# Masking in the scan of a stick-breaking mixer, and transposes in halves of 64 rows, in a two-layer decoder kernel

## The chip, the cores and the metric

The kernel runs on one core of a Trainium2 chip. A core has a matrix engine (TensorE, PE in the profile; its weight loads are listed apart as PEld), a vector engine (VectorE, DVE), a scalar engine (ScalarE, ACT), a general engine (GpSimd, POOL) and a queue engine that starts transfers (SyncE, SP). Each takes its instructions in order from a queue of its own and waits on semaphores for results of the others. Operands lie in SBUF; TensorE writes to PSUM, which has 8 banks of 128 partitions by 512 fp32 numbers, and ScalarE and VectorE read them from there. The metric is the device time of one execution in microseconds; lower is better.

## What is computed

A decoder of two layers on 512 tokens with 1024 features, all in float32. Each layer is a feed-forward half step, a mixer and a second feed-forward half step, each on a normed input; a final norm closes it. The first layer's mixer is a gated linear attention, the second one's (the one changed here) a stick-breaking attention of 16 heads with 64 features. The part that the change touches, cut to its core:

```python
z = jnp.einsum('bhtd,bhsd->bhts', q_blk, k).astype(jnp.float32) * scale
mask = s_pos[None, :] < t_pos[:, None]
sp = jnp.where(mask, jax.nn.softplus(z), 0.0)
rem = lax.cumsum(sp, axis=3, reverse=True) - sp
weights = jnp.where(mask, jnp.exp(jax.nn.log_sigmoid(z) - rem), 0.0)
return jnp.einsum('bhts,bhsd->bhtd', weights.astype(v.dtype), v)
```

A token t may look at tokens s < t alone. Since log_sigmoid(z) = z - softplus(z), the exponent is z minus the sum of softplus from s up to t - 1, taken from the right. For the second edit only the end matters: the last feed-forward half step is added to x, and each token's row is divided by its root mean square and scaled by `final_norm`.

## The kernel before

**Layout.** Activations lie feature by feature: `xs[0..7]`, each 128 features by 512 tokens. A float32 product is made of three products in a rounded format: an operand is cut into a high part (ScalarE's cast, L152 for weights `wh`) and a remainder (VectorE's subtraction, L153, `wl`), and `mm3` adds high x high, low x high and high x low. So each weight tile costs ScalarE and VectorE an instruction before TensorE can use it. Weights come from HBM through SP's queue.

**Order.** The program is a list of entries in `feed.q`, each a generator that issues some products and yields (a "half"). `feed.halves(k)` runs k such pieces, and starting an entry cuts the weights of the next ones ahead of their use. The engines' queues are filled by the framework, which places instructions by their dependences and priorities; `tc.issue_after` holds an instruction behind another. PSUM banks come from four rotating sets ("a" 2 banks, "z" 3, "t" 2, "o" 1). Where no set is named they rotate through all 8, so that the ninth request takes the bank of the first.

**The mixer (class SB).** `run` goes through 17 steps. Step s < 16 makes the logits of one head (`weights_log`); step s > 0 makes the weights of the head of the step before (`weights`: transposes, Exp), and every second step the products with the values (`values`) of a pair of heads. Between them `feed.halves` puts pieces of the projection products that make the next heads' queries, keys and values. So TensorE alternates between a head's own work and projections.

A head's logits (512 queries by up to 512 keys, causal) lie in three banks: `bk` 1 holds query tile 2 (384 columns), `bk` 2 the tiles 1 and 0 (384), `bk` 0 tile 3 (512). For each bank:

- TensorE: two products per query tile (L1484 in `logits`, key high and key low), and a mask product: `idb` (identity, bf16) times `negm` (-1e30 at and right of the diagonal), which adds the mask to the diagonal 128 x 128 block. In steps 0 to 4 it comes behind the logits; from step 5 on (`AHEAD`) `masks` lays the masks of banks 1 and 2 for the next step ahead, as the first write of the bank.
- ScalarE: `l` = |z| (L1527), Exp(-l) and Ln(1 + l) (both through `act`, L656), and `r` = Relu(z) (L1530). r + l is softplus(z), and 0 where masked.
- VectorE: the scan (L1533) runs from right to left in SBUF, state = (r + state) + l, one for each query tile; then r = z - l (L1541), z once more from PSUM, which is the exponent.

`st["relu"]` marks the last Relu; `parts` places the casts of later queries and keys (`mq`, `kh`, L1478) behind it. `weights` then transposes r (L1555, `ps_T`), takes Exp (`wt`) and `values` multiplies (L1570, `ps_oT`).

**The end.** `to_tokens` runs in the last feed-forward half step, ahead of its last product `back_tok` (`ps_bt`). It turns `xs` from feature by feature to token by token: for each half of the features (`hf`) it takes four banks, one for each token tile i, transposes 4 x 4 blocks of 128 x 128 with the block as the stationary operand and `ident` as the moving one (L1650), and ScalarE copies each bank of 512 columns (L1655) into `xt[i, hf]`, which takes the place of `xs`. The first `ps_bt` is the ninth request and takes the first of these eight banks. `last` (L1665) adds the product to `xt`.

Of the kernel before, what the change touches and what calls it, by code (L numbers as in the profile page):

```python
# [23 lines left out]
NT = T // P  # L24
EPS = 1e-6
LEVELS = (64, 32, 16, 8, 4, 2, 1)
NEG = -1.0e30

def turns(t):

    return t.rearrange("p (two n) -> p n two", two=2)
# [13 lines left out]
def decoder(ctx: ExitStack, tc: tile.TileContext, a: dict, out: bass.AP):  # L47
    nc = tc.nc
# [28 lines left out]
    xs = [xp.tile([P, T], F32, name=f"x{k}") for k in range(KD)]  # L77
# [449 lines left out]
    st = {}  # L527
# [102 lines left out]
    def two_halves(between=None):  # L630

        feed.finish()
        g = [feed.start(), feed.start()]
        for i in range(3):
            for n, x in enumerate(g):
                next(x, None)
                next(x, None)
                if between is not None and (i, n) == (1, 0):
                    between((recent[-4], recent[-1]))

    def new_norm():
        st["h"], st["l"], st["made"] = st["nh"], st["nl"], range(KD)
# [6 lines left out]
    def exp_ln_tables(after):  # L649
        with tc.issue_after(after):  # L650
            st["tab"] = nc.scalar.preload_act_table_set("natural_log_exp_and_others").ins

    def act(o, i, fn, **kw):

        with tc.issue_after(st["tab"]):
            st["last"] = nc.scalar.activation(o, i, fn, **kw).ins  # L656
# [744 lines left out]
    class SB:  # L1401
# [81 lines left out]
        def logits(self, o_, l_, r_, first, last=False):  # L1483
            nc.tensor.matmul(o_, l_, r_, start=first, stop=last, skip_group_check=True)  # L1484

        def mask(self, bk, ps, first):

            w = self.WID[bk]
            m0 = P if bk == 2 else w - P
            nb = (w - m0) // P  # L1490
            self.logits(
                ps[:, m0:w].rearrange("p (n s) -> p n s", n=nb),
                self.idb,
                self.negm.unsqueeze(1).to_broadcast([P, nb, P]),
                first,
                not first,
            )

        def masks(self, s):


            if self.AHEAD <= s < 16:
                for bk in (1, 2):
                    self.zs[bk] = psum("ps_z", "z")
                    self.mask(bk, self.zs[bk], True)

        def weights_log(self, p, e):

            m = self.qk[p, e, "q"]
            kh, kl = self.qk[p, e, "k"]  # L1510
            self.ys[p, e] = ys = [None] * 3
            for bk, tiles in ((1, (2,)), (2, (1, 0)), (0, (3,))):
                ahead = bk in self.zs
                ps = self.zs.pop(bk) if ahead else psum("ps_z", "z")
                w = self.WID[bk]
                for n_, i in enumerate(tiles):

                    c0, n = self.BK[i][1], max(2, i + 1) * P
                    ts_ = slice(i * P, (i + 1) * P)
                    o_, h_, l_ = ps[:, c0 : c0 + n], turns(kh)[:, 0 : n // 2], turns(kl)[:, 0 : n // 2]  # L1520
                    self.logits(o_, m[:, ts_], h_, n_ == 0 and not ahead)
                    self.logits(o_, m[:, ts_], l_, False, ahead and i == tiles[-1])
                if not ahead:
                    self.mask(bk, ps, False)
                r = self.hp.tile([P, w], F32, tag=f"r{bk}", name="r")
                l = self.hp.tile([P, w], F32, tag=f"l{bk}", bufs=1, name="l")
                nc.scalar.activation(l, ps[:, 0:w], AF.Abs)  # L1527
                act(l, l, AF.Exp, scale=-1.0)
                act(l, l, AF.Ln, bias=1.0)
                st["relu"] = nc.scalar.activation(r, ps[:, 0:w], AF.Relu).ins  # L1530
                for i in tiles:
                    c = slice(self.BK[i][1], self.BK[i][1] + (i + 1) * P)
                    nc.vector.tensor_tensor_scan(  # L1533
                        out=l[:, c][:, ::-1],
                        data0=r[:, c][:, ::-1],
                        data1=l[:, c][:, ::-1],
                        initial=0.0,
                        op0=ALU.add,
                        op1=ALU.add,
                    )  # L1540
                nc.vector.tensor_tensor(out=r, in0=ps[:, 0:w], in1=l, op=ALU.subtract)  # L1541
                ys[bk] = r
                yield

# [38 lines left out]
        def run(self):  # L1583
            with ExitStack() as es:
                vp = es.enter_context(tc.tile_pool(name="vp2", bufs=1, reuse_waits="tile"))
                self.op = es.enter_context(tc.tile_pool(name="op", bufs=8, reuse_waits="tile"))
                self.qp = es.enter_context(tc.tile_pool(name="qp2", bufs=4, reuse_waits="tile"))
                self.hp = es.enter_context(tc.tile_pool(name="hp3", bufs=2, reuse_waits="tile"))
                self.v = [vp.tile([P, D], F32, name=f"w{i}") for i in range(NT)]
                self.ys, self.wt, self.zs = {}, {}, {}  # L1590
                self.later, self.hold = [], False
                self.idb = vp.tile([P, P], BF16, name="idb")
                self.negm = vp.tile([P, P], BF16, name="negm")
                nc.vector.tensor_copy(self.idb, ident)
                nc.gpsimd.dma_start(self.negm, a["c_neg"])
                new_norm()
                two_halves()
                stats_a("t")
                feed.step(2)
                stats_b("t")  # L1600
                exp_ln_tables(st["sqrt"])
                flush(self.defer)
# [37 lines left out]
    xt = {}  # L1640

    def to_tokens(tp):
        st["tp"] = tp
        fin = st["fin"] = tp.tile([P, D], F32, tag="s", bufs=4, name="fin")
        nc.gpsimd.dma_start(fin, a["final_norm"].partition_broadcast(P))
        for hf in range(2):
            ps = [psum("ps_T") for _ in range(NT)]
            for m in range(4):
                for i in range(NT):
                    nc.tensor.transpose(  # L1650
                        ps[i][:, m * P : (m + 1) * P], xs[hf * 4 + m][:, i * P : (i + 1) * P], ident
                    )
            for i in range(NT):
                xt[i, hf] = xs[hf * 4 + i]
                nc.scalar.copy(xt[i, hf], ps[i])  # L1655

        with tc.issue_after(st["updated"]):
            nc.vector.tensor_scalar(out=fin, in0=fin, scalar1=2.0 * float(D) ** 0.5, scalar2=None, op0=ALU.mult)
# [308 lines left out]
def _constants():  # L1967
# [29 lines left out]
```

## Time and profile before

| what | value |
|---|---|
| three runs, median (lowest to highest) | 1760.18 us (1759.73 to 1760.69) |
| the profiled execution: time, span | 1759.99 us, 1758.0 us |
| granted TensorE clock, mean | 0.999 |
| busy over the span: PE, DVE, ACT, POOL | 99%, 86%, 61%, 3% |
| the mixer's first and last logits (L1484) | 1220.5 and 1384.7 us |
| transposes of the end (L1650), 32 | 1726.8 to 1730.2 us |

The profile is of one execution. Times in it count from the start of the span. A busy share says how long an engine had an instruction in work; matmuls overlap their neighbours, so their distance from start to start is their cost, not their duration. The "chain of waits" follows the work back from the last instruction to what released it. In a row of groups, "x48 | 25.4, 529" is the count, the busy time in us and the mean in ns, and behind the second bar stands the idle time of the engine in front of these instructions and who ended it.

### The profile page before, as it was taken

What the parts mean: (1) busy time and instruction counts of PE and PEld (TensorE: products, weight loads), DVE (VectorE), ACT (ScalarE), POOL (GpSimd) and SP (SyncE); (2) the same over time, 40 slices, a digit from 0 to 9 for tenths busy, and PEclk for the clock granted to TensorE, in tenths of its full rate; (3) what the DMA queues carried; (4) which work ended last, traced back from release to release, by engine and by line L of the source; (5) the groups of instructions that cost most, each with busy time, mean ns of one, the idle gap of its engine ahead of it and who ended that gap; (6) DMA issues with size and microseconds to landing.
All of it is one profiled execution on the core that took longest, in us unless ns stands there. A gap on an engine that the chain in (4) does not pass through costs nothing.

```text
span 1758.0 us, 31376 instructions
## 1 busy us (share of the span) xinstructions
PE 1746.1 (99%) x12714; PEld 1630.1 (93%) x12714; DVE 1509.0 (86%) x2490; ACT 1064.3 (61%) x1903; POOL 55.6 (3%) x77
## 2 busy tenths in 40 slices
PE   9999999999999999999999999999999999999998
PEld 8999999889888999999989999999888889999997
DVE  8999797786888999889798988977898679998886
ACT  7556555555655556555556555655888755555555
POOL 0000000200000000000000000010000000000000
PEclk9999999999999999999999999999999999999999
DMA  5533435412123433444434334352212234434351
GB/s 168 156 112 118 131 110 144 120 56 82 57 93 99 132 109 121 120 121 127 134 94 133 106 123 135 101 132 84 85 49 73 72 96 133 132 97 125 117 148 51
DMA packets 186388, 193.14 MB, mean 110 GB/s; under 512 B 4930, under 2 KB 171124, under 8 KB 186244
## 3 DMA queue, kind: packets, MB, share of 16 engines
q1 hardware_dynamic: 177760, 175.91, 32.0%
q0 software_dynamic: 8240, 14.95, 4.7%
q8 instruction: 99, 1.62, 0.4%
q14 instruction: 45, 0.37, 0.1%
q10 hardware_dynamic: 244, 0.29, 0.0%
HBM read 175.17 MB, written 2.10 MB: 101 GB/s over the span
## 4 chain that ended last, share of the span: by engine, by line
PE 90%; DVE 6%; ACT 3%; issue 1%; DMA 1%; DVEq 0%; SPq 0%
PE ps_w L779 21%; PE ps_d L80 15%; PE ps_f L80 15%; PE ps_q L779 10%; PE ps_z L779 5%; PE ps_t L80 5%; PE ps_w L412 5%; PE ps_b L80 4%; PE ps_q L412 2%; DVE wl L153 1%; PE ps_z L1484 1%; PE ps_z L412 1%; PE ps_oT L1570 1%; PE ps_bt L80 1%; PE ps_T L1555 1%
## 5 line engine op out<-in xcount | busy, mean ns | idle before, releaser
L153 DVE TENSOR_TENSOR wl<-raw,wh 128x1024 fp32r<-128x1024 f32 x241 | 255.5, 1061 | 37.6 <-ACT wh L152 36.6
L152 ACT CAST wh<-raw 128x1024 fp32r<-128x1024 f32 x241 | 222.2, 922 | 72.3 <-PE ps_f L80 27.4
L153 DVE TENSOR_TENSOR wl<-s,wh 128x1024 fp32r<-128x1024 f32 x160 | 195.4, 1221 | 66.4 <-ACT wh L152 65.5
L779 PE MATMUL ps_w<-th,wh 128*128 128x256 f32 x864 | 239.1, 277 | 0.3 <-ACT ps_z L807 0.3
L779 PE MATMUL ps_w<-tl,wh 128*128 128x256 f32 x864 | 237.8, 275 | 0.0
L779 PE MATMUL ps_w<-th,wl 128*128 128x256 f32 x864 | 237.8, 275 | 0.0
L152 ACT CAST wh<-s 128x1024 fp32r<-128x1024 f32 x160 | 168.9, 1055 | 6.0 <-DVE s L765 6.0
L779 PEld LDWEIGHTS ps_w<-th,wh 128*128 128x128 f32 x864 | 165.9, 192 | 1.1 <-ACT ps_z L807 0.5
L80 PE MATMUL ps_f<-xh,wh 128*128 128x512 f32 x432 | 166.4, 386 | 0.0
L779 PEld LDWEIGHTS ps_w<-tl,wh 128*128 128x128 f32 x864 | 166.0, 192 | 0.0
L779 PEld LDWEIGHTS ps_w<-th,wl 128*128 128x128 f32 x864 | 165.9, 192 | 0.0
L80 PE MATMUL ps_f<-xh,wl 128*128 128x512 f32 x432 | 164.1, 380 | 0.5 <-DVE wl L153 0.5
L80 PE MATMUL ps_f<-xl,wh 128*128 128x512 f32 x432 | 163.9, 379 | 0.0
L80 PE MATMUL ps_d<-hh,wh 128*128 128x512 f32 x416 | 157.9, 379 | 0.0
L80 PE MATMUL ps_d<-hl,wh 128*128 128x512 f32 x416 | 157.8, 379 | 0.0
L80 PE MATMUL ps_d<-hh,wl 128*128 128x512 f32 x416 | 157.8, 379 | 0.0
L153 DVE TENSOR_TENSOR wl<-rawd,wh 128x1024 fp32r<-128x1024 f32 (+1 forms) x100 | 96.3, 963 | 9.3 <-ACT wh L152 9.3
L807 ACT COPY ps_z<-ps_w 128x256 f32<-128x256 f32 x72 | 26.0, 362 | 118.1 <-PE ps_w L779 117.8
L363 POOL DMA_DIRECT2D x<-d x53 | 45.9, 911 | 1550.3 <-ACT d L362 1092.2
L80 PEld LDWEIGHTS ps_f<-xh,wl 128*128 128x128 f32 x432 | 81.9, 189 | 11.3 <-DVE wl L153 0.9
L80 PEld LDWEIGHTS ps_f<-xl,wh 128*128 128x128 f32 x432 | 81.8, 189 | 11.3
L80 PEld LDWEIGHTS ps_f<-xh,wh 128*128 128x128 f32 x432 | 81.9, 190 | 10.6
(357 smaller groups left out, 5427.8 us busy)
## 6 DMA issues: line engine op xcount, KB each, us to landing
raw<-in_ffn_w_gate_dram SPq DMA_DIRECT2D x43, 1024.0 KB, 5.4
raw<-in_ffn_w_up_dram SPq DMA_DIRECT2D x43, 1024.0 KB, 5.4
rawd<-in_ffn_w_down_dram SPq DMA_DIRECT2D x84, 512.0 KB, 3.8
x<-d POOLq DMA_DIRECT2D x53, 256.0 KB, 4.5
raw<-in_gla_w_in_dram SPq DMA_DIRECT2D x12, 1024.0 KB, 5.3
raw<-in_sb_w_in_dram SPq DMA_DIRECT2D x16, 512.0 KB, 3.7
raw<-in_gla_w_out_dram SPq DMA_DIRECT2D x4, 1024.0 KB, 4.9
raw<-in_sb_w_in_dram SPq DMA_DIRECT2D x4, 1024.0 KB, 5.2
```

The costliest lines, as they stand in the source:

```text
L80: st["pe"] = nc.tensor.matmul(ps, l, r, start=first, stop=last).ins
L152: nc.scalar.copy(h[:, k], part)
L153: nc.vector.tensor_tensor(out=l[:, k], in0=part, in1=h[:, k].bitcast(F32), op=ALU.subtract)
L363: nc.gpsimd.dma_start(xs[k], d, accum_op=ALU.add)
L412: st["pe"] = nc.tensor.matmul(ps, l_, r_, start=first and c + n == 0, stop=c == 1 and n == 2, skip_group_check=True).ins
L779: st["pe"] = nc.tensor.matmul(o, l_, r_, start=first and j + n == 0, stop=j == 3 and n == 2, skip_group_check=True).ins
L807: v["copied"] = nc.scalar.copy(z, w).ins
L1484: nc.tensor.matmul(o_, l_, r_, start=first, stop=last, skip_group_check=True)
L1555: nc.tensor.transpose(ps[:, c0 : c0 + P], ys[yb][:, yc + j * P : yc + (j + 1) * P], ident)
L1570: nc.tensor.matmul(po[e * 64 : e * 64 + 64, j * P : T], self.v[j][:, c : c + 64], self.wt[p, e][bk][:, c0 : c0 + n], start=j == 0, stop=j ...
```

## The change

**Mixer.** The mask products, `idb`, `negm` and its load, `mask` and `masks` are gone. ScalarE copies the logits out of the bank into `r`; VectorE bounds `r` at 44 in place; ScalarE takes `l` = Exp(r) and Ln(1 + l), which is softplus without the detour by |z|. The mask moves into the scan: a new tile `keep` (128 x 512) holds 1 everywhere but for a 0 in each row where s = t - 1, and the scan is state = keep x state + l from the right, starting at 1e30. Up to the diagonal the state stays 1e30, at s = t - 1 it starts anew with l. The exponent r - l is then -1e30 for masked keys. The subtraction reads `r` from SBUF, so the bank is no longer needed after the copy. `parts` now waits for the last Ln.

**End.** A block is transposed in two halves: 64 of its 128 rows (features) by 128 tokens, with 64 x 64 of `ident` as moving operand, into a 128 x 64 piece. The two halves use the upper and the lower 64 partitions of their operands and go to two different banks; a bank holds one half of two token tiles. The loop goes over token tiles first and the four blocks within, and ScalarE makes two copies of 256 columns for a token tile in place of one of 512.

```diff
-        def mask(self, bk, ps, first):
...
-        def masks(self, s):
...
-                ahead = bk in self.zs
-                ps = self.zs.pop(bk) if ahead else psum("ps_z", "z")
+                ps = psum("ps_z", "z")
...
-                    self.logits(o_, m[:, ts_], h_, n_ == 0 and not ahead)
-                    self.logits(o_, m[:, ts_], l_, False, ahead and i == tiles[-1])
-                if not ahead:
-                    self.mask(bk, ps, False)
+                    self.logits(o_, m[:, ts_], h_, n_ == 0)
+                    self.logits(o_, m[:, ts_], l_, False, i == tiles[-1])
...
-                nc.scalar.activation(l, ps[:, 0:w], AF.Abs)
-                act(l, l, AF.Exp, scale=-1.0)
+                nc.scalar.copy(r, ps[:, 0:w])
+                nc.vector.tensor_scalar(out=r, in0=r, scalar1=TOP, scalar2=None, op0=ALU.min)
+                act(l, r, AF.Exp)
                 act(l, l, AF.Ln, bias=1.0)
-                st["relu"] = nc.scalar.activation(r, ps[:, 0:w], AF.Relu).ins
+                st["logs"] = st["last"]
                 for i in tiles:
                     c = slice(self.BK[i][1], self.BK[i][1] + (i + 1) * P)
                     nc.vector.tensor_tensor_scan(
                         out=l[:, c][:, ::-1],
-                        data0=r[:, c][:, ::-1],
+                        data0=self.keep[:, T - (i + 1) * P :][:, ::-1],
                         data1=l[:, c][:, ::-1],
-                        initial=0.0,
-                        op0=ALU.add,
+                        initial=-NEG,
+                        op0=ALU.mult,
                         op1=ALU.add,
                     )
-                nc.vector.tensor_tensor(out=r, in0=ps[:, 0:w], in1=l, op=ALU.subtract)
+                nc.vector.tensor_tensor(out=r, in0=r, in1=l, op=ALU.subtract)
...
-                self.idb = vp.tile([P, P], BF16, name="idb")
-                self.negm = vp.tile([P, P], BF16, name="negm")
-                nc.vector.tensor_copy(self.idb, ident)
-                nc.gpsimd.dma_start(self.negm, a["c_neg"])
+                self.keep = vp.tile([P, T], F32, name="keep")
+                nc.gpsimd.memset(self.keep, 1.0)
+                c = slice(T - P - 1, T - 1)
+                nc.vector.tensor_scalar(
+                    out=self.keep[:, c], in0=ident, scalar1=-1.0, scalar2=1.0, op0=ALU.mult, op1=ALU.add
+                )
...
-                                self.parts(st["relu"])
+                                self.parts(st["logs"])
...
-                            if i == 1:
-                                self.masks(s + 1)
...
-            ps = [psum("ps_T") for _ in range(NT)]
-            for m in range(4):
-                for i in range(NT):
-                    nc.tensor.transpose(
-                        ps[i][:, m * P : (m + 1) * P], xs[hf * 4 + m][:, i * P : (i + 1) * P], ident
-                    )
+            ps = [psum("ps_T").rearrange("p (i m c) -> p i m c", i=2, c=64) for _ in range(NT)]
+            halves = slice(0, 64), slice(64, P)
+            for i in range(NT):
+                for m in range(4):
+                    x = xs[hf * 4 + m][:, i * P : (i + 1) * P]
+                    for n, r in enumerate(halves):
+                        nc.tensor.transpose(ps[i // 2 * 2 + n][:, i % 2, m], x[r], ident[r, r])
             for i in range(NT):
                 xt[i, hf] = xs[hf * 4 + i]
-                nc.scalar.copy(xt[i, hf], ps[i])
+                to = xt[i, hf].rearrange("p (m n c) -> p n m c", n=2, c=64)
+                for n in range(2):
+                    nc.scalar.copy(to[:, n], ps[i // 2 * 2 + n][:, i % 2])
```

More of the change, by code (lines that the diff above doesn't have):

```diff
@@ L27 @@
 NEG = -1.0e30
+TOP = 44.0
 def turns(t):
@@ L1484, in logits @@
             nc.tensor.matmul(o_, l_, r_, start=first, stop=last, skip_group_check=True)
-        def mask(self, bk, ps, first):
[L1488 to L1496, printed above, removed]
-            )
-        def masks(self, s):
[L1502 to L1505, printed above, removed]
         def weights_log(self, p, e):
@@ L1589, in run @@
                 self.v = [vp.tile([P, D], F32, name=f"w{i}") for i in range(NT)]
-                self.ys, self.wt, self.zs = {}, {}, {}
+                self.ys, self.wt = {}, {}
                 self.later, self.hold = [], False
-                self.idb = vp.tile([P, P], BF16, name="idb")
-                self.negm = vp.tile([P, P], BF16, name="negm")
-                nc.vector.tensor_copy(self.idb, ident)
-                nc.gpsimd.dma_start(self.negm, a["c_neg"])
+                self.keep = vp.tile([P, T], F32, name="keep")
[4 more added lines that the diff above has]
+                )
                 new_norm()
@@ L1646, in to_tokens @@
         for hf in range(2):
-            ps = [psum("ps_T") for _ in range(NT)]
-            for m in range(4):
-                for i in range(NT):
-                    nc.tensor.transpose(
-                        ps[i][:, m * P : (m + 1) * P], xs[hf * 4 + m][:, i * P : (i + 1) * P], ident
-                    )
+            ps = [psum("ps_T").rearrange("p (i m c) -> p i m c", i=2, c=64) for _ in range(NT)]
[5 more added lines that the diff above has]
+                        nc.tensor.transpose(ps[i // 2 * 2 + n][:, i % 2, m], x[r], ident[r, r])
             for i in range(NT):
                 xt[i, hf] = xs[hf * 4 + i]
-                nc.scalar.copy(xt[i, hf], ps[i])
+                to = xt[i, hf].rearrange("p (m n c) -> p n m c", n=2, c=64)
+                for n in range(2):
+                    nc.scalar.copy(to[:, n], ps[i // 2 * 2 + n][:, i % 2])
         with tc.issue_after(st["updated"]):
```

## The prediction

> **What bounds the kernel now.** I read the page first, then the busy time by stretches, then the groups of the softmax mixer, the time order of single engines there, and last the time order at the final feed-forward.
>
> ```profile
> span 1758.0 us, 31376 instructions
> ...
> PE 90%; DVE 6%; ACT 3%; issue 1%; DMA 1%; DVEq 0%; SPq 0%
> ```
>
> TensorE holds 90% of the chain that ended last. So an edit pays where it takes matmuls out of TensorE's stream, and costs where it makes another engine late for that stream. The mixer's weight loop runs from about 1216 to 1400 us. By stretches:
>
> ```profile
> core 0: us, PE busy (x) PEld busy (x) DVE busy (x) ACT busy (x) POOL busy (x), PEclk, DMA share, GB/s
> 1226.00:1372.00 146.00, 145.52 (x956) 123.07 (x955) 129.26 (x188) 130.01 (x263) 0.00 (x0) 1.00 0.23 69
> 242.00:264.00 22.00, 22.00 (x199) 22.00 (x198) 22.00 (x41) 12.84 (x24) 0.00 (x0) 1.00 0.31 97
> ```
>
> In 1226 to 1372 all three engines are heavily used: TensorE 145.5 of 146 us, VectorE 129.3 (89%), ScalarE 130.0 (89%). VectorE is idle for 16.7 us there. The row of 242 to 264 us, from another stage, shows that VectorE can be busy for 22.0 of 22 us without a gap on TensorE, so long as its results are wanted late.
>
> **The mask matmuls go.** 48 of them run (3 banks in 16 steps). Busy time is modelled and overlaps, so I take the distance from a mask's start to that of the next matmul.
>
> ```profile
> L1484 PE MATMUL ps_z<-negm,idb x48: 229/230/284, 1221.1 to 1385.1; 128*128 128x128 bf16 x32, 128*128 128x256 bf16 x16
> ...
> 1221.63 0.28 PE L1484 MATMUL ps_z<-negm,idb 128*128 128x256 bf16 x1
> 1221.67 0.46 PE L80 MATMUL ps_f<-xh,wh 128*128 128x512 f32 x1
> ...
> 1328.67 0.34 PE L1484 MATMUL ps_z<-negm,idb 128*128 128x128 bf16 x2
> 1328.84 0.38 PE L1555 MATMUL ps_T<-ident,r 128*128 128x128 f32 x2
> ...
> 1290.53 0.23 PE L1484 MATMUL ps_z<-negm,idb 128*128 128x128 bf16 x1
> 1290.59 0.61 PE L1555 MATMUL ps_T<-ident,r 128*128 128x128 f32 x4
> ```
>
> A mask behind its own logits takes 0.04 us, the two laid ahead together 0.17, the third one 0.06. Steps 0 to 4 lay none ahead: 5 x 3 masks at about 0.05 = 0.75 us. Steps 5 to 15: 11 x (0.17 + 0.06) = 2.5 us. Sum **3.3 us**, all in a stream with next to no gaps, so it comes off the time as long as nothing else is late.
>
> **ScalarE and VectorE in a bank.** Before, a bank costs ScalarE Abs, Exp, Ln and Relu, and VectorE the scan and the subtraction. After, ScalarE does a copy, Exp and Ln; VectorE does the new bound at 44, the scan and the subtraction.
>
> ```profile
> L1530 ACT ACTIVATE r<-ps_z 128x384 f32<-128x384 f32 x32 | 15.7, 490 | 0.0
> L1530 ACT ACTIVATE r<-ps_z 128x512 f32<-128x512 f32 x16 | 9.7, 608 | 0.0
> ```
>
> Then VectorE's nearest rows, one constant operation on SBUF first, the scan and the subtraction of now behind:
>
> ```profile
> L1318 DVE TENSOR_SCALAR vv<-vv 128x512 f32<-128x512 f32 x4 | 1.7, 423 | 0.0
> L1658 DVE TENSOR_SCALAR fin<-fin 128x1024 f32<-128x1024 f32 x1 | 0.7, 685 | 0.0
> ...
> L1533 DVE TENSOR_TENSOR_SCAN l<-r,l 128x512 f32<-128x512 f32 x16 | 19.5, 1219 | 4.5 <-ACT l L656 4.5
> L1541 DVE TENSOR_TENSOR r<-ps_z,l 128x384 f32<-128x384 f32 x32 | 17.8, 558 | 1.8
> ```
>
> ScalarE: the copy costs what the Relu or the Abs cost (same bank, same width), so one of four goes: 15.7 + 9.7 = 25.4 us over the stage. It gains nothing by itself, since ScalarE is not the bound, but its waits become fewer.
>
> VectorE: the bound is one constant operation from SBUF to SBUF. 512 columns take 423 ns and 1024 take 685, so 384 come to an estimated 423 - 128 x (685 - 423)/512 = 357 ns. Over the stage 32 x 0.357 + 16 x 0.423 = **18.2 us** more. From below it might be about 0.3 us where instructions overlap at their ends (14 us); from above, 0.558 like the subtraction (28 us). I take 18.2, its rows being the same operation. The scan takes 2.4 ns a column (1219/512); with a multiplication in place of the first addition I leave it there, because its two operands and its feedback stay. The subtraction now reads SBUF instead of PSUM; I count no gain.
>
> How many banks lie in 1226 to 1372 is told by the subtraction's busy time there, one a bank:
>
> ```profile
> 1226.00:1372.00 146.00, 24.72 (x41) 1.00 0.23 69
> ```
>
> 41 of 48, two of three with 384 columns. VectorE there: 129.3 + 27 x 0.357 + 14 x 0.423 = **144.9 us**. TensorE would need 146 - 41/48 x 3.3 = **143.2 us**. So VectorE goes from 89% to just past TensorE, and falls 1.7 us behind over the stretch even without a wait. That is the point on which the forecast hangs. What lets it be late is the distance of a step's last subtraction from its reader, and the waits that may go:
>
> ```profile
> 1287.71 0.69 DVE L1541 TENSOR_TENSOR r<-ps_z,l 128x512 f32<-128x512 f32 x1
> ```
>
> ```profile
> DVE l L1533 <- ACT l L656: 10.5, 12, 1.4
> ...
> DVE wl L153 <- ACT wh L152: 5.2, 4, 2.1
> ```
>
> A step's last subtraction ends at 1288.4; the transposes that read it start at 1290.59 (above). So results are wanted 2.2 us after they exist. And 15.7 us of VectorE's waits in the stage, in these two rows alone, are on ScalarE, which is to lose a sixth of its work. I take one wait of a scan, of the longest size (1.4), as left on top of the 1.7: 3.1 late, 2.2 of it covered, **0.9 us given back** to TensorE.
>
> The new wait: Exp in ScalarE's queue now waits for the bound, and behind it stand the casts `wh` (L152) and `mq`, `kh` (L1478), for which VectorE's `wl`, `mq`, `kl` and then TensorE wait. ScalarE is idle for 16 us of the 146, and loses 27 x 0.49 + 14 x 0.608 = 21.7 us of Relu: 37.7 us for 41 banks, 0.9 us a bank, before such waits make it late. The bound itself takes 0.36 to 0.42, so I count nothing.
>
> The preparation (a memset on POOL, one 128 x 128 operation on VectorE against the 128 x 128 cast of `idb`) replaces a DMA issue and that cast. I count nothing; a wait of VectorE for the memset, with the norm's statistics queued behind it, could cost about 1 us (my allowance). The bank of the logits comes free at the copy instead of at the subtraction; no wait for it is worth counting now.
>
> **The last transposes.**
>
> ```profile
> 1726.79 3.66 PE L1650 MATMUL ps_T<-ident,x 128*128 128x128 f32 x32
> 1730.20 0.46 PE L80 MATMUL ps_bt<-wh,hh 128*128 128x512 f32 x1
> ```
>
> ScalarE and VectorE at the same place (first reader of the copies last):
>
> ```profile
> 1727.04 1.05 ACT L152 CAST wh<-raw 128x1024 fp32r<-128x1024 f32 x1 [1.98 <-PE ps_d L80]
> 1728.41 4.01 ACT L1655 COPY x<-ps_T 128x512 f32<-128x512 f32 x8 [0.31 <-PE ps_T L1650]
> ...
> 1733.14 0.69 DVE L1665 SCALAR_TENSOR_TENSOR x<-ps_bt,x 128x512 f32<-128x512 f32 x1 [3.57 <-PE ps_bt L80]
> ```
>
> And the nearest rows for halves and for copies of half the width:
>
> ```profile
> 380.88 0.69 PE L80 MATMUL ps_S<-q,k 128*64 128x64 f32 x16
> ...
> L807 ACT COPY ps_z<-ps_w 128x256 f32<-128x256 f32 x72 | 26.0, 362 | 118.1 <-PE ps_w L779 117.8
> ```
>
> 32 transposes take 3.41 us to the next product, 0.107 each. After, each is two of 64 rows and 64 columns. No row shows halves by rows; the nearest are halves by columns (`ps_S`): 16 matmuls with 64 columns each start within 0.69 less their last one's 0.22, so a pair takes about 0.06 us. At that pace 32 pairs take 1.9 us, and some 0.2 for going into and out of halves is my allowance; TensorE would be ready at 1728.9. From above, halves that do not overlap at all and still cost 0.107 each take 6.8 us, 3.4 more than now.
>
> But the first `ps_bt` takes the bank of the first pair of transposes, which now comes free only after three of 16 copies. ScalarE's cast ends at 1728.1; a copy of 256 columns takes 0.362: 1728.1 + 3 x 0.362 = 1729.2, with the signal 1729.3. So the product starts 0.9 us earlier than 1730.20: **-0.9 us** (from -1.4, if the copies pass the cast, to +3.4). The 16 copies end by 1728.1 + 5.8 = 1733.9, but the addition at 1733.14 wants the first two only.
>
> On halves the Trainium skill speaks against the change: "TensorE: Matmul & The Clock Gate", section "LDWEIGHTS (loading the stationary operand)", says that a load's time follows its columns, not its rows, some 107 ns for 128 columns. By it 32 overlapped pairs would still take 3.4 us and the gain of 0.9 would be gone; that belongs to the third rival. Two loads of full transposes in this trace stand in the way of that figure:
>
> ```profile
> L1650 PEld LDWEIGHTS ps_T<-ident,x x32: 138/141/146, 1726.6 to 1730.1; 128*128 128x128 f32 x32
> ...
> 4.80 0.20 PEld L1779 LDWEIGHTS ps_x<-ident,x 128*128 128x128 f32 x2 [0.50 <-DMA x<-in_x_dram]
> ```
>
> Two take 0.20 us together at 0.14 each, so the second started 0.06 after the first.
>
> **The sum**, on the profiled execution's own 1759.99 us (span 1758.0 and 2.0 around it; the three runs' median is 1760.18, 0.2 above): 1759.99 - 3.3 + 0.9 - 0.9 = 1756.7. I forecast **1756.6 us**, the last tenth for ScalarE's fewer waits. Its own range is 1753.6 (nothing given back, copies early, the few waits of transposes on ScalarE gone too) to 1759.
>
> **Rivals.**
> *VectorE becomes the bound of the mixer* (slower). Place: 1226 to 1372. It decides as soon as VectorE's unavoidable idle time there exceeds some 3 us: 144.9 of work leaves 1.1 below the old 146, and 2.2 are covered. For: 89% plus 11% is all there is, and the bound stands in front of an Exp that stands in front of a scan. Against: the idle time now comes mostly from ScalarE, which gets lighter. If half of today's 16.7 us of idle stays: 144.9 + 8.4 - 2.2 - 146 = +5.1, outside the stretch -0.5, transposes -0.9: 1763.7. If a quarter stays, 1759.5; if all, 1772.
> *ScalarE stalls at the bound* (slower). Place: Exp behind the bound in each bank, when the bound sits behind a `wl`, VectorE's longest instruction there. It decides beyond 0.9 us a bank. At a mean of 1.1: 0.2 x 41 = +8.2, so 1756.6 + 8.2 = 1764.8. Against: ScalarE's other work can be ordered in between.
> *The halves do not overlap, or their loads take as long as whole ones*: the change does not do there what it says. The tail's gain is 0 to -3.4: 1757.5 to 1760.9.
>
> **How the numbers follow.** Forecast 0.50, VectorE the bound 0.30, ScalarE stalled 0.08, halves that do not pay 0.12. A measurement of this kernel tells about 0.2% (3.5 us) from no change, so faster means under 1756.7 and slower over 1763.7. Of the forecast's 0.50, 0.35 lies below 1756.7; of the halves' 0.12, 0.05, when the mixer gives back nothing: faster 0.40. Of VectorE's 0.30 half lies over 1763.7 and of ScalarE's 0.08 nearly all with a little from elsewhere: slower 0.25. The rest, 0.35, is within 0.2%. The range is 1753.5 to 1767: its lower end is that of the forecast, its upper end VectorE with three quarters of its idle time left (1767.8).
>
> **What would show it.** Right: no `negm` rows and 48 fewer matmuls; `r` with 48 new VectorE rows near 0.36 and 0.42 us; the scan still 2.4 ns a column; TensorE's stretch from the first to the last logits 2 to 3 us shorter; `ps_T` of the last stage over in 2 us and `ps_bt` about 0.9 us earlier in relation to it. Wrong: waits of TensorE on VectorE's `r`, `wl` or `kl` in the mixer, VectorE busy over 97% there; or Exp rows waiting for `r` with `wh` late; or pairs of transposes whose starts lie 0.1 us apart. A scan that costs more with the multiplication, by a tenth (0.12 us on one of 512 columns), would by itself tip the forecast to the first rival.

## The result, and the profile after

| kernel | median (lowest to highest) | runs |
|---|---|---|
| before | 1760.19 us (1759.73 to 1760.69) | 6 |
| after | 1774.57 us (1771.65 to 1777.16) | 6 |

The change makes the kernel slower by 0.8%: the ratio of after to before is 1.008, 95% interval 1.007 to 1.0091. The forecast was 1756.6 us, within 1753.5 to 1767. The profiled execution of after took 1777.16 us, the slowest of its six, so terms that are read from it add up to some 2.6 us more than the median shows.

The head of the page of after, to set beside the one of before:

```profile
span 1775.2 us, 31315 instructions
...
PE 87%; DVE 9%; ACT 3%; issue 1%; DMA 0%; DVEq 0%; ACTq 0%
```

TensorE holds 87% of the chain in place of 90%, VectorE 9% in place of 6%. To see where the 17.2 us of span came in, the same instructions are found in both traces. First the single lines of after (count, shortest, median and longest duration in ns, first and last start in us): the last small operation ahead of the mixer, and the products with the values, whose last one ends the mixer.

```profile
L595 DVE TENSOR_SCALAR dg<-ident,r x8: 279/280/286, 349.2 to 1209.3; 128x128 f32<-128x128 f32 x8
...
L1548 PE MATMUL ps_oT<-wt,w x128: 272/486/844, 1255.2 to 1418.4; 128*64 128x512 f32 x32, 128*64 128x384 f32 x32, 128*64 128x256 f32 x32, 128*64 128x128 f32 x32
```

And of before:

```profile
L594 DVE TENSOR_SCALAR dg<-ident,r x8: 280/282/287, 347.4 to 1207.4; 128x128 f32<-128x128 f32 x8
...
L1570 PE MATMUL ps_oT<-wt,w x128: 272/432/644, 1251.4 to 1399.2; 128*64 128x512 f32 x32, 128*64 128x384 f32 x32, 128*64 128x256 f32 x32, 128*64 128x128 f32 x32
```

Ahead of the mixer after is 1.9 us late (1.7 of it from the first 20 us, where nothing was changed), at its end 19.2. So **the mixer lost 17.3 us**, where the forecast had 2.4 gained. The end, time order on TensorE of after (start, duration):

```profile
1745.24 2.21 PE L1631 MATMUL ps_T<-ident,x 64*128 64x64 f32 x64
1747.38 0.48 PE L81 MATMUL ps_bt<-wh,hh 128*128 128x512 f32 x1
```

The last transposes start 18.5 us later than in before (1726.79), so 0.7 came back between the mixer and the last transposes; where is not shown. From the first transpose to the first `ps_bt` it takes 2.14 us in place of 3.41: the second edit gives **1.3 us**, and 17.2 remain to the end.

Now the mixer of after, busy time by stretches:

```profile
core 0: us, PE busy (x) PEld busy (x) DVE busy (x) ACT busy (x) POOL busy (x), PEclk, DMA share, GB/s
1216.00:1416.00 200.00, 187.17 (x1108) 157.62 (x1108) 165.82 (x267) 139.78 (x265) 0.00 (x0) 0.97 0.21 64
1226.00:1372.00 146.00, 137.22 (x812) 115.93 (x811) 128.03 (x207) 106.78 (x205) 0.00 (x0) 0.96 0.20 62
```

The same stage of before:

```profile
1216.00:1400.00 184.00, 183.04 (x1162) 152.78 (x1161) 152.60 (x216) 155.96 (x314) 0.00 (x0) 1.00 0.24 74
```

TensorE, idle for 1.0 us before, is now idle for 12.8, and its clock is no longer full. No engine is full: VectorE is busy for 128.0 of 146 us, a little less than before (129.3; the same 146 us now hold less of the mixer), and ScalarE for 107. Work that fits and yet comes late points to waits. The waits of after from 1200 to 1420 us (engine and line, what it waited for, us in all, times, longest):

```profile
ACT l L657 <- DVE r L1505: 32.6, 28, 3.2
DVE l L1511 <- ACT l L657: 19.7, 23, 1.4
...
PEld ps_oT L1548 <- ACT wt L657: 9.8, 7, 3.0
```

The first row did not exist before: ScalarE's Exp (`l`, through `act`, L657) stands idle for 32.6 us because VectorE's bound (L1505) has not come. VectorE's scan then waits for ScalarE, and TensorE for `wt`, the Exp of the step before, which stands in ScalarE's queue behind the waiting one. The bound itself is as short as forecast, and the scan as long (groups of after):

```profile
L657 ACT ACTIVATE l<-r 128x512 f32<-128x512 f32 x16 | 10.1, 630 | 18.4 <-DVE r L1505 18.2
...
L1505 DVE TENSOR_SCALAR r<-r 128x384 f32<-128x384 f32 x32 | 10.3, 352 | 0.7 <-ACT r L1504 0.3
L1505 DVE TENSOR_SCALAR r<-r 128x512 f32<-128x512 f32 x16 | 6.6, 410 | 0.0
...
L1511 DVE TENSOR_TENSOR_SCAN l<-keep,l 128x512 f32<-128x512 f32 x16 | 19.6, 1223 | 8.9 <-ACT l L657 8.9
```

So why does ScalarE wait for an instruction of 0.41 us? One bank in order of time, ScalarE first:

```profile
1253.34 0.57 ACT L1504 COPY r<-ps_z 128x512 f32<-128x512 f32 x1
1253.80 0.53 ACT L657 ACTIVATE l<-l 128x384 f32<-128x384 f32 x1
1254.23 0.59 ACT L657 ACTIVATE wt<-ps_T 128x512 f32<-128x512 f32 x1
1254.70 0.84 ACT L1427 ACTIVATE w<-ps_t,r 128x256 f32<-128x256 f32 x2
1258.04 0.63 ACT L657 ACTIVATE l<-r 128x512 f32<-128x512 f32 x1 [2.49 <-DVE r L1505]
1258.58 0.58 ACT L657 ACTIVATE wt<-ps_T 128x512 f32<-128x512 f32 x1
```

VectorE meanwhile:

```profile
1253.96 0.54 DVE L1519 TENSOR_TENSOR r<-r,l 128x384 f32<-128x384 f32 x1
1254.51 0.42 DVE L1467 CAST kl<-kl 64x512 fp32r<-64x512 f32 x1
1254.95 0.42 DVE L1465 CAST kh<-n 64x512 fp32r<-64x512 f32 x1
1255.40 0.69 DVE L1466 TENSOR_TENSOR kl<-n,kh 64x512 fp32r<-64x512 f32 x1
1256.12 0.69 DVE L1511 TENSOR_TENSOR_SCAN l<-keep,l 128x256 f32<-128x256 f32 x1
1256.83 0.42 DVE L1467 CAST kl<-kl 64x512 fp32r<-64x512 f32 x1
1257.26 0.42 DVE L1511 TENSOR_TENSOR_SCAN l<-keep,l 128x128 f32<-128x128 f32 x1
1257.60 0.40 DVE L1505 TENSOR_SCALAR r<-r 128x512 f32<-128x512 f32 x1
```

And TensorE, with one such place later on:

```profile
1255.24 1.72 PE L1548 MATMUL ps_oT<-wt,w 128*64 128x512 f32 x6
1259.21 2.50 PE L1548 MATMUL ps_oT<-wt,w 128*64 128x384 f32 x10 [2.25 <-ACT wt L657]
...
1307.90 1.54 PE L1548 MATMUL ps_oT<-wt,w 128*64 128x256 f32 x6 [2.59 <-ACT wt L657]
```

The copy is done at 1253.9. The bound starts 3.7 us later, at 1257.60, since VectorE takes its queue in order and has seven other instructions to do first. ScalarE, also in order, does four other instructions until 1255.5 and then stands idle for 2.49 us until the Exp at 1258.04; the `wt` behind it begins at 1258.58, and TensorE, which needs that `wt`, stands still for 2.25 us. Over all 48 banks of this trace the median from the end of the copy to the start of the bound is 1.3 us; from the end of the bound to the start of Exp it is 0.03.

A gap costs more than its own length. The stretches in and behind these two gaps, clock in the third column from the end:

```profile
1257.00:1259.00 2.00, 0.00 (x0) 0.00 (x0) 1.46 (x4) 0.96 (x2) 0.00 (x0) 1.00 0.00 0
1259.50:1262.50 3.00, 3.00 (x13) 1.77 (x10) 2.05 (x3) 1.03 (x3) 0.00 (x0) 0.51 0.00 0
1263.00:1266.00 3.00, 3.00 (x28) 3.00 (x27) 1.55 (x4) 2.81 (x7) 0.00 (x0) 1.00 0.02 5
1307.50:1314.00 6.50, 6.09 (x19) 4.77 (x20) 5.20 (x10) 3.58 (x9) 0.00 (x0) 0.50 0.20 56
```

At the end of the first gap TensorE is granted half its clock, for all of the 3 us of the second row, and with the second gap for all of the 6.5 us of the last row. (Whole lengths, and a third such stretch, stand in the last section.) The Trainium skill, "TensorE: Matmul & The Clock Gate", section "What's actually happening", says that the clock is either full or half, set by the activity in free-running windows of about 3.4 us; the halves, and their lengths of about one and two such windows, agree. By the same section the clock falls after an idle window, also about 3.4 us; here idle times of 2.25 and 2.59 us were enough.

Added up for the profiled execution: 11.8 us more idle time on TensorE and some 6 us through the clock (0.03 of 200, a rounded share), less 3.3 us of mask products saved, come to 14.5 of the 17.3 us. The rest I can't place; the busy time of matmuls is modelled, so idle time read from it is not exact.

The transposes of the end, rows of `ps_T` in after:

```profile
L1631 PEld LDWEIGHTS ps_T<-ident,x x64: 134/140/142, 1745.2 to 1747.2; 64*128 64x128 f32 x64
L1631 PE MATMUL ps_T<-ident,x x64: 222/223/273, 1745.2 to 1747.2; 64*128 64x64 f32 x64
```

64 loads in 2.0 us are 0.062 us a pair. The formula of the Trainium skill for a load ("TensorE: Matmul & The Clock Gate", section "LDWEIGHTS (loading the stationary operand)"), by which 128 columns take an estimated 107 ns, would make 3.4 us of 32 pairs if only the two loads of a pair ran side by side. These rows do not bear that out, though a single load of 64 rows is listed at 140 ns, as long as one of 128 rows before (141).

### The profile page after: what moved, and what is told of

Same layout as the page of the kernel before. It is cut to its first block, busy times and chain, and to the rows that moved or that the text cites. A ratio compares the mean times of both kernels' runs of the same rounds, so it can differ in the third digit from the quotient of the medians.

```text
span 1775.2 us, 31315 instructions
## 1 busy us (share of the span) xinstructions
PE 1752.5 (99%) x12698; PEld 1634.6 (92%) x12698; DVE 1521.7 (86%) x2538; ACT 1048.8 (59%) x1863; POOL 55.7 (3%) x77
## 4 chain that ended last, share of the span: by engine, by line
PE 87%; DVE 9%; ACT 3%; issue 1%; DMA 0%; DVEq 0%; ACTq 0%
PE ps_w L780 22%; PE ps_d L81 15%; PE ps_f L81 12%; PE ps_q L780 11%; PE ps_z L780 5%; PE ps_w L413 5%; PE ps_b L81 4%; PE ps_t L81 3%; PE ps_q L413 2%; DVE l L1511 2%; ACT l L657 1%; DVE wl L154 1%; PE ps_z L413 1%; PE ps_bt L81 1%; DVE r L1519 1%; PE ps_S L81 1%
## 5 line engine op out<-in xcount | busy, mean ns | idle before, releaser
L81 PEld LDWEIGHTS ps_f<-xl,wh 128*128 128x128 f32 x432 | 82.0, 190 | 11.7
```

Of the source, the lines that this page charges most:

```text
L81: st["pe"] = nc.tensor.matmul(ps, l, r, start=first, stop=last).ins
```

## The experiments

Three theories of the loss stood against each other. **The wait:** ScalarE's chain copy, Exp, Ln now runs through VectorE's queue and back, and waits there. **The work:** VectorE has 17 us more to do and becomes the bound of the mixer. **The rest:** something else in the change costs time (the last transposes, the scan with its new operand, the earlier release of the bank).

**The second edit alone.** Before, with only the transposes changed.

> The kernel before with the second edit alone (the last transposes in halves). In the profile of the changed kernel the distance from the mixer's end to the first ps_bt is 2.05 us shorter than before. If that is the edit's own gain: 1760.2 - 2.0 = 1758.2 us. If it is something that only goes with the changed mixer (a lag caught up there): 1760.2, within 0.5. In both cases the mixer's stretch is that of before, so the first edit alone costs what is left: about 16 us.

Measured: 1758.91 us (1758.09 to 1760.73) beside 1759.88 of before, ratio 0.9992 (0.9983 to 1.0001). Its profile shows the same 2.14 us as after:

```profile
1726.72 2.22 PE L1653 MATMUL ps_T<-ident,x 64*128 64x64 f32 x64
1728.86 0.48 PE L80 MATMUL ps_bt<-wh,hh 128*128 128x512 f32 x1
```

The trace has a gain of 1.3 us at that place, the runs 1.0, which by themselves can't be told from none. That lies between the two values expected. The transposes start at 1726.72 us here and at 1726.79 in before, so the 0.7 us that came back ahead of them in after go with the changed mixer. The loss is not here.

**The bound aside.** All of VectorE's new work stays, but nobody on ScalarE waits for it; the logits that Exp sees are not bounded.

```diff
                 nc.scalar.copy(r, ps[:, 0:w])
                 nc.vector.tensor_scalar(out=r, in0=r, scalar1=TOP, scalar2=None, op0=ALU.min)
-                act(l, r, AF.Exp)
+                act(l, ps[:, 0:w], AF.Exp)
```

> The changed kernel, but Exp reads the logits from the bank and not the bounded copy; copy, bound and subtraction stay. VectorE has the same work (48 bounds, 17 us), and nothing on ScalarE waits for the bound any more. Theory, ScalarE stalls at the bound (32.6 us of waits of Exp on r in the changed kernel): the waits are gone and the time falls to 1760.2 - 3.3 - 2.0 = 1755, up to 1758 if VectorE's extra work shows. Rival, VectorE's throughput: the same 17 us of work fill the same stretch, so it stays within 3 us of the changed kernel's 1774.6.

Measured: 1752.73 us (1752.43 to 1753.26) beside 1759.88, ratio 0.9956 (0.9943 to 0.997): 21.8 us below after, and faster than before. Its stretch:

```profile
1226.00:1372.00 146.00, 145.48 (x937) 126.05 (x936) 141.81 (x234) 116.27 (x231) 0.00 (x0) 1.00 0.23 69
```

VectorE is busy for 141.8 of 146 us, 97%, far above the 128.0 of after, and TensorE is idle for only 0.5 us at full clock. An engine at 97% delays nobody here, as long as nobody waits for each single result. That is against the work and for the wait. (The time is below the range that was expected, as it is in the next two runs; see "Missed on the other side" below.)

**No bound.** The line L1505 taken out; logits not bounded.

> The changed kernel without the bound at 44 (logits are not bounded): VectorE's 17 us and the wait are both gone; copy, Exp, Ln, scan and subtraction stay. Both theories (stall, throughput): 1755, with 1754 to 1757. A third, that the new order of the queues or the lost masks laid ahead cost the time and the bound has no part in it: over 1765.

Measured: 1751.96 us (1751.56 to 1752.32), ratio 0.9951 (0.9938 to 0.9965). Beside the bound aside, 17 us of VectorE's work are worth 0.8 us (the two also differ in what Exp reads, `r` or the bank).

**The bound on ScalarE.** 44 - Relu(44 - z) is the smaller of z and 44, so ScalarE can bound while it copies, and no other engine is in the chain. `self.top` is a column of 44.

```diff
-                nc.scalar.copy(r, ps[:, 0:w])
-                nc.vector.tensor_scalar(out=r, in0=r, scalar1=TOP, scalar2=None, op0=ALU.min)
-                act(l, r, AF.Exp)
+                nc.scalar.activation(r, ps[:, 0:w], AF.Relu, bias=self.top, scale=-1.0)
+                act(l, r, AF.Exp, bias=self.top, scale=-1.0)
...
-                nc.vector.tensor_tensor(out=r, in0=r, in1=l, op=ALU.subtract)
+                nc.vector.tensor_tensor(out=r, in0=r, in1=l, op=ALU.add)
...
-                act(t, ps[:, 0:w], AF.Exp)
+                act(t, ps[:, 0:w], AF.Exp, bias=self.top, scale=-1.0)
```

> The same function with the bound on ScalarE: Relu(44 - z) from the bank in place of the copy, Exp(44 - that), Ln; VectorE scans and adds, and the last Exp takes 44 minus its argument. No bound on VectorE, no wait of ScalarE on it; each of the three ScalarE instructions of a bank but Ln has a per-partition constant. Theory (stall) and rival (throughput) both: 1755 to 1758; over 1760 if the constants make ScalarE's instructions so much longer that it becomes the bound.

Measured: 1753.32 us (1753.10 to 1753.73), ratio 0.9959 (0.9946 to 0.9973). The whole function of after, 21.3 us faster than after and 6.6 faster than before. This is the version to keep.

**The wait without the work.** The bound touches 16 columns of each bank only; the rest of the logits is not bounded.

```diff
-                nc.vector.tensor_scalar(out=r, in0=r, scalar1=TOP, scalar2=None, op0=ALU.min)
+                nc.vector.tensor_scalar(out=r[:, 0:16], in0=r[:, 0:16], scalar1=TOP, scalar2=None, op0=ALU.min)
```

> The changed kernel with the bound on 16 columns of each bank alone (the others are left unbounded): Exp still waits for an instruction in VectorE's queue, but VectorE's work for it is some 48 x 0.16 = 8 us in place of 17. Theory, the wait is what costs (it counts by the place in the queue, not by the length): 1768 to 1775. Rival, VectorE's work: half of the loss gone or more, under 1763.

Measured: 1773.47 us (1770.59 to 1774.77) beside 1760.31, ratio 1.0073 (1.0058 to 1.0088). The bound shrinks to less than half, and the wait does not (waits, then groups):

```profile
ACT l L657 <- DVE r L1505: 33.8, 24, 3.6
```

```profile
L1505 DVE TENSOR_SCALAR r<-r 128x16 f32<-128x16 f32 x48 | 6.8, 165 | 0.5
```

10.1 of 16.9 us of work taken away, 1.2 us of 14.4 won back. This and the bound aside are the two halves of the proof: all of the work without the wait costs 0.8 us, the wait with 40% of the work costs 13.2. In this kernel's profiled run the clock was 1.00 from 1226 to 1372 us and 0.50 for 3.4 us at 1389, which is some 1.7 us, and the mixer still lost 13.9 us; so most of the loss does not need the slower clock.

**The bound first in VectorE's queue.** The bound is issued at a higher priority.

```diff
-                nc.vector.tensor_scalar(out=r, in0=r, scalar1=TOP, scalar2=None, op0=ALU.min)
+                with ahead():
+                    nc.vector.tensor_scalar(out=r, in0=r, scalar1=TOP, scalar2=None, op0=ALU.min)
```

> The changed kernel with the bound given priority, so that it is placed in VectorE's queue as early as its copy allows. Same work, same wait. Theory, the wait is long because the bound stands behind other work in VectorE's queue: Exp's 32.6 us of waits fall to under 12 (0.25 a bank) and the time to 1754 to 1760. If the queue order stays as it is, or one VectorE instruction in front is enough to do the harm: over 1768.

Measured: 1768.57 us (1768.08 to 1769.08), ratio 1.0047 (1.0032 to 1.0062). The median from the copy to the bound falls from 1.3 to 0.8 us, but its mean only from 1.4 to 1.2, and ScalarE's wait from 32.6 to 29.8, where under 12 was expected. 6 of the 14.4 us come back all the same. All four runs read a mean clock of 0.999 and the median run of after 0.997; 0.002 of 1770 us is 3.5 us. So much of the gain is the clock, which no gap halves in this kernel's mixer, and little of it a shorter wait. The priority did not take the other work out of the bound's way.

**VectorE reads the bank.** No copy on ScalarE; the bound goes from PSUM straight into `r`, so the chain crosses between ScalarE and VectorE once less.

```diff
-                nc.scalar.copy(r, ps[:, 0:w])
-                nc.vector.tensor_scalar(out=r, in0=r, scalar1=TOP, scalar2=None, op0=ALU.min)
+                nc.vector.tensor_scalar(out=r, in0=ps[:, 0:w], scalar1=TOP, scalar2=None, op0=ALU.min)
```

> The changed kernel without ScalarE's copy: VectorE bounds the logits straight from the bank into r. One hop fewer for Exp (VectorE to ScalarE in place of ScalarE to VectorE to ScalarE), ScalarE relieved by 24 us, VectorE's bound near the subtraction's 0.56 and 0.69 from the bank: 48 of them 29 us, 12 more than in the changed kernel. If the wait in VectorE's queue is what costs: still 1765 to 1778, as Exp waits there as before. If the two hops with ScalarE's copy are what costs: under 1760.

Measured: 1777.17 us (1776.74 to 1778.47), ratio 1.0097 (1.0082 to 1.0112), as slow as after or slower. Its waits:

```profile
ACT l L657 <- DVE r L1504: 48.5, 28, 3.1
```

Its groups:

```profile
L1504 DVE TENSOR_SCALAR r<-ps_z 128x384 f32<-128x384 f32 x32 | 16.9, 550 | 7.2 <-PE ps_z L1485 7.1
```

The wait grows from 32.6 to 48.5 us: ScalarE no longer has the copy to do meanwhile, and the bound's row of 384 columns takes 550 ns from PSUM in place of 352. One crossing less wins nothing as long as Exp still waits for VectorE.

**No masks.** Before, with the mask products left out and nothing in their place; no masking is done.

> The kernel before without its mask products and without laying them ahead (keys at and right of the diagonal are not masked); everything else is as before. The prediction's 3.3 us for 48 masks: 1756.6. The stretch of the mixer in the kernels without the wait is 4.9 to 6.0 us shorter than before; if masks alone make that up, 1754 to 1755.

Measured: 1756.55 us (1755.58 to 1758.60), ratio 0.9978 (0.9969 to 0.9988), 3.8 us below its before; the mixer in its trace is 3.2 us shorter. The forecast's term for the masks was 3.3.

**The bound aside, twice.** The bound's line stands twice in the kernel of the bound aside, to see where work alone begins to cost.

> As the kernel whose Exp reads the bank (nothing on ScalarE waits for the bound), with the bound done twice: VectorE gets 17 us more once again. That kernel had VectorE at 141.8 of 146 us in 1226 to 1372; the second bound brings its work there to about 156. If VectorE can be the mixer's bound at all, this is past the point: 8 to 14 us slower than that kernel's 1752.7, so 1761 to 1767. If the lag is made up elsewhere: under 1757.

Measured: 1762.08 us (1761.44 to 1763.04) beside 1760.21, ratio 1.001 (1.0001 to 1.002), 9.3 us above the bound aside. Its mixer:

```profile
1216.00:1400.00 184.00, 178.04 (x1092) 151.22 (x1091) 176.21 (x311) 133.63 (x263) 0.00 (x0) 1.00 0.23 69
```

VectorE is now busy for 176.2 of 184 us, 96%, and TensorE idle for 6.0. So the work theory is right about a limit, but it lies between the 17 us that the change adds and twice as much.

**Neither copy nor bound.** ScalarE's Exp and VectorE's subtraction both read the bank; logits not bounded.

> The changed kernel without copy and without bound (logits are not bounded): Exp and the subtraction read the bank. ScalarE has two instructions a bank, VectorE what it had before the change. If TensorE alone sets the mixer once nothing waits: as the kernel without the bound, 1752.0 within 1; if ScalarE's 24 us less still help: 1750 to 1751; if the bank held to the subtraction now delays the logits: over 1753.5.

Measured: 1753.46 us (1752.30 to 1754.43), ratio 0.9961 (0.9946 to 0.9976), the same as with the copy (1751.96) or a little slower; the intervals overlap, and none of the three cases expected is met clearly. Taking 24 us of copies off ScalarE (14.5 and 9.2 in the groups of after) wins nothing. Whether the copy gives something by releasing the bank earlier is not shown by 1.5 us.

## Why the prediction was wrong

**The step that failed** is the one on the new wait: ScalarE would become late only beyond 0.9 us a bank, "the bound itself takes 0.36 to 0.42, so I count nothing". It failed in two places. First, it set the duration of the bound in the place of the time until its result is there. That time is the wait in VectorE's queue plus the duration: 1.3 us at the median plus 0.35 to 0.41, about 1.7 us from the end of the copy. ScalarE has other work in part of it; what is left is 32.6 us of idle time in front of Exp, where the forecast has none. Second, the limit was an average. 32.6 us over 48 banks are 0.7 a bank, less than the 0.9 that the sentence allows, and yet TensorE came late: the idle time comes in 28 pieces of up to 3.2 us, at places where ScalarE's queue holds nothing more ahead of Exp, and one such piece of 2.49 us is enough to stop TensorE for 2.25. The rows for the first point were there: VectorE was busy for 89% of the stretch, so an instruction that becomes ready finds others ahead of it, whose rows (a scan of 512 columns 1.22 us, `wl` as long) are several times the bound's.

**The chance of 0.08** for "ScalarE stalls at the bound" rested on "ScalarE's other work can be ordered in between". The bank at 1253 us shows what was in between: four instructions, which filled 1.6 of the 4.1 us between the copy's end and Exp; nothing was left for the other 2.5. The rival named the mechanism and its place rightly. Its point of decision, 0.9 us a bank, was wrong as above, and its price, 8.2 us, came from a mean of 1.1 us a bank taken by assumption; the measured time is 18.0 us above the forecast.

**VectorE as the bound**, the rival with 0.30, is refuted as the cause: VectorE has a smaller busy share in after than in before, and at 97% in the bound aside TensorE is not late. Its sum was arithmetic on busy time with an assumed share of idle time; that idle time is not a property of VectorE, it comes from who waits for whom. The point itself exists, as the doubled bound shows.

**The halves that do not pay** (0.12) are refuted by 2.14 us for the 32 pairs, against 3.41 for the whole blocks.

**What held.** The sign it named for a wrong forecast came true: Exp rows waiting for `r`. The masks: 3.3 us forecast, 3.2 in the mixer's trace without them and 3.8 (2.1 to 5.5 by the interval) in the runs. The bound's duration: 0.357 and 0.423 forecast, 0.352 and 0.410 measured. The scan unchanged at 2.4 ns a column. The pace of the halves: 0.06 us a pair.

**Mis-sized, in the right direction:** the last transposes gave 1.3 us in place of 0.9. The bound of that term was to be the bank, held until the third of 16 copies. In after the sixteen copies take 4.51 us, 0.28 each from start to start, where 0.362 was taken from a row of durations, and the first `ps_bt` starts with no wait for the bank:

```profile
1746.36 4.51 ACT L1636 COPY x<-ps_T 128x256 f32<-128x256 f32 x16
```

**Missed on the other side:** with the wait gone the change gains 6.6 to 8 us, not 3.4. The mixers of the bound aside and of the bound on ScalarE are 5.6 and 4.9 us shorter than before's, of which the masks explain 3.2. What gives the other 2 is not shown by any run. The lighter chain on ScalarE, argued for at the low end of the range, is one candidate; against it, the kernel with neither copy nor bound is lighter still and no faster. That low end, 1753.6, does not follow from its own terms: 1759.99 - 3.3 - 1.4 is 1755.3, and the 1.7 us of waits that are still missing are more than TensorE's whole idle time in the mixer of before, 1.0 us.

**The size** is mostly explained once the clock is set apart. Four kernels have an Exp that waits: after, 16 columns, priority and the one that reads the bank. Their waits are 32.6, 33.8, 29.8 and 48.5 us, and their mixers are 17.3, 13.9, 10.1 and 20.2 us longer than before's. In these mixers TensorE had half its clock for 13.7, 3.4, 0 and 17.1 us. Half of that time taken off as lost, an estimate, leaves 10.5, 12.2, 10.1 and 11.7 us. So the waiting Exp costs 10 to 12 us in each, net of the masks saved, and the rest of the spread is the clock. **Open** is why 48.5 us of wait cost no more than 30: which wait delays TensorE depends on what stands behind it, and no run separates that bank by bank.

## What to carry to other kernels

An instruction put on another engine in the middle of a chain costs that engine's queue, not its own duration: price it as the time until its turn comes (here 1.3 us at the median, up to 3.7, for 0.4 of work), and ask what stands behind the instruction that waits for it. Spare time averaged over a stage does not tell whether such a wait fits: here 0.7 us a bank did harm where 0.9 was free on average. VectorE with 97% of its time in use was harmless where its results were wanted late, and costly at 88% where each result was wanted at once; so move work off a chain, or keep the chain on one engine even when its instruction is longer there (the bound by Relu on ScalarE). To tell a cost of work from a cost of waiting, run both halves apart: the work with no one waiting, and the wait with next to no work.

## What the runs showed of the hardware

Gaps of 2.25, 2.59 and 2.15 us on TensorE brought its granted clock to half, for 3.4, 6.8 and 3.4 us, in a run whose mean over the whole run still reads 0.995. The three stretches at half clock begin at 1259.57, 1307.35 and 1392.68 us, which are 14 and 25 times 3.413 us apart. So in this trace the clock changes on a grid of 3.41 us. The pieces of the grid just ahead of them:

```profile
1256.15:1259.57 3.42, 1.17 (x7) 0.33 (x5) 2.30 (x5) 1.53 (x3) 0.00 (x0) 1.00 0.00 0
1303.94:1307.35 3.41, 1.38 (x8) 0.42 (x4) 3.33 (x7) 3.21 (x5) 0.00 (x0) 1.00 0.17 53
1389.27:1392.68 3.41, 1.26 (x8) 0.88 (x7) 2.27 (x5) 2.50 (x6) 0.00 (x0) 1.00 0.00 0
```

TensorE is idle for 2.25, 2.03 and 2.15 us of them. In the kernel with the bound on 16 columns the half clock begins at 1388.90 us; the grid laid through that point gives these pieces:

```profile
1255.78:1259.19 3.41, 1.41 (x10) 0.96 (x10) 3.16 (x5) 2.22 (x6) 0.00 (x0) 1.00 0.00 0
1300.16:1303.57 3.41, 1.86 (x10) 0.56 (x6) 2.47 (x5) 2.33 (x4) 0.00 (x0) 1.00 0.49 144
1303.57:1306.98 3.41, 1.96 (x14) 1.61 (x15) 3.29 (x7) 2.43 (x6) 0.00 (x0) 1.00 0.04 12
1385.49:1388.90 3.41, 1.01 (x5) 0.90 (x6) 2.16 (x4) 3.41 (x8) 0.00 (x0) 1.00 0.00 0
```

Its longest gap, 3.00 us at 1302, falls into two pieces with 1.55 and 1.45 us of idle time, and the clock stays full; so it does after a piece with 2.00 us, and a piece with 2.40 is followed by half. In the kernel whose bound reads the bank, the pieces ahead of its three stretches at half clock have 3.00, 2.80 and 2.21 us. So in these traces it is not the length of a gap that decides but the idle time within one piece of the grid, with the line at about 2 of 3.41 us. The grid does not lie at the same place in each run (from 1259.57 in after to 1388.90 in the run with 16 columns is 37.9 pieces, no whole number), so whether a gap halves the clock can differ from run to run, and with it the time: the six runs of after spread over 5.5 us, with 0.995 of the clock in the slowest and 0.998 in the fastest; 0.003 of 1775 us is 5.3 us. The six of before, a kernel without such gaps in the mixer, spread over 1.0 us.

Two transposing loads of 64 rows in the upper and lower half of the array, each 0.14 us long, follow the pair before them by 0.062 us; whole loads of 128 rows, also 0.14 us long, follow each other by 0.107.
